# One core, a macaron block (FFN, mLSTM with RG-LRU, FFN): x loaded first, a new ramp, mixer squares on ScalarE, adaLN rates by section, two tiles kept for the end

## The chip, the cores and the metric

One core of one Trainium2 chip. The metric is the device time of one execution in microseconds (us); the core's engines are TensorE (PE in the profile, its weight loads PEld), VectorE (DVE), ScalarE (ACT), GpSimd (POOL) and SyncE (SP, which issues most DMA loads).

## The reference

The input x has 256 rows (tokens) of 2048 float32 values; everything is float32. The block is three sublayers, each modulated by a vector c (adaLN):

```python
mod = (silu(c) @ w_ada + b_ada).reshape(3, 3, 2048)          # shift, scale, gate of each sublayer
def modulate(h, s): return layer_norm(h) * (1 + scale[s]) + shift[s]

y = swiglu(modulate(x, 0), ffn1_w13, ffn1_w2)                # (silu(u@wg) * (u@wv)) @ w2, inner width 5632
x = layer_norm(ALPHA*x + 0.5*gate[0]*y, ln_g[0], ln_b[0])
u = modulate(x, 1)
q, k, v, o, i, f, x_rg, g_rg = split(u @ w_in + b_in)
h_m = layer_norm(mlstm(q, k, v, i, f)) * mlstm_norm_g * sigmoid(o)     # 4 heads of 256
x_rg = causal_depthwise_conv(x_rg, width 4)
h_r = rg_lru(x_rg, ...) * gelu(g_rg)                          # gates in 8 blocks of 128, recurrence over time
y = concat(h_m, h_r) @ w_out
x = layer_norm(ALPHA*x + gate[1]*y, ln_g[1], ln_b[1])
y = swiglu(modulate(x, 2), ffn2_w13, ffn2_w2)
x = layer_norm(ALPHA*x + 0.5*gate[2]*y, ln_g[2], ln_b[2])
```

## The kernel before

**Weights.** Each weight matrix is cut into tiles of 1 MB (128 partitions x 2048 float32). A tile is loaded on SP's queue into one of four `raw` buffers (L86). ScalarE casts it to a rounded `hi` part (L96), VectorE forms `lo` = raw - hi (L98), and each product is three matmuls: hi by hi, lo by hi, hi by lo (L638 to L640 in the ramp, L289 to L291 elsewhere). The tiles' names are `r`, `h` or `l` with a section behind: `rra7`, `hra7`, `lra7` are the three forms of ramp tile 7; `rs` belongs to the mixer's projections, `rv` and `ro` to v and o, `rwo` to the output projection. The hi and lo tiles have three buffers each.

**adaLN.** The product of silu(c) with `w_ada` is done on VectorE: 144 tiles of 1 MB, called `ada0` to `ada143`, are loaded through the same queue and the same four `raw` buffers, and each takes one multiply-and-sum (L174, "the reduce") that leaves 128 numbers of shift, scale or gate in `adac`. They are spread over the program by a rate: each load of a weight tile adds the rate of the section to a credit, and each whole credit loads an adaLN tile (`tick`). Where a value is needed, `ada_until` issues all that lead to it at once. So the constants `RAMP_RATE`, `FFN1_RATE`, `MIX_RATE` and `FFN2_RATE` place these tiles.

**Start and ramp.** x comes in four pieces; VectorE takes the statistics of each half of the rows (`stx`, `mvx`), GpSimd the inverse deviation (`vex`, `rsx`), ScalarE normalizes (`n`, L1092). TensorE transposes 128-column blocks of n (L243, bank `tu`); ScalarE applies scale and shift (L247) and rounds (L250), VectorE forms the low part (L251): that is u, one "k-tile" per 128 columns, 16 in all. The first part of FFN1, the ramp, does 16 units of 512 columns with only the first k-tiles, then with the next, and so on: `STAGES` = (2, 4, 5, 5) k-tiles. A stage of k k-tiles reads 4 k weight tiles. In each stage, `modulate` of the next stage's k-tiles stands ahead of unit 14. Partial sums of units 0 and 1 stay in PSUM (`kp`); the others go to SBUF, by ScalarE copies in stage 0 (L673) and by VectorE adds later (L675).

**Mixer.** After a boundary (final take of y, layer norm, next u) come the sections o, x (with the convolution, L899 and L902), g (the RG gates L910 to L913, the recurrence L919 to L929, its output L937 to L944), v, k, then q with the four heads (L978 to L1016) and the output projection. The heads' decay weights are in `misc`.

**Tail.** After FFN2's last group, `boundary` finishes the two halves of the rows one after the other: `products(t)` adds the last weight tiles into four banks per half (`tl20n`, `tl21n`), `take` multiplies by the gate, adds to x and takes statistics, `norm` writes the layer norm and the output.

**Order.** A scheduler orders each engine's instructions by a simulated timeline; engines wrapped in `Pinned` (V, A, G, T) keep program order.

## Time and profile before

| what | value |
|---|---|
| median of 3 runs | 1959.12 us (1951.45 to 1960.45) |
| the profiled execution | 1956.92 us, its span 1955.1 us |
| TensorE busy | 1881.4 us, 96% |
| VectorE, ScalarE, GpSimd busy | 1425.5, 847.8, 43.3 us |
| granted TensorE clock, mean | 0.988 |
| DMA | 515.87 MB, mean 264 GB/s |

The span runs from the first to the last instruction of the trace. In a row of the timeline the numbers are start and duration in us; a bracket gives the idle time of the engine ahead of the instruction and what ended it. In a group's row they are total busy time and the mean of one in ns, then the idle time before them.

### The profile page before, as it was taken

The page shows a single profiled execution, that of the slowest core. Times are in us where ns is not written, and L with a number is a line of the kernel's source. Part 1 is how long each engine was busy: PE and PEld are TensorE (multiplying, and loading weights), DVE is VectorE, ACT ScalarE, POOL GpSimd, SP SyncE. Part 2 cuts the span into 40 slices and gives each one's busy share as a digit, 9 for nine tenths or more (in the row PEclk, how much of TensorE's full clock was granted, in tenths as well). Part 3 has the DMA queues.
Part 4 walks back from the last instruction along what each step waited for, and adds up shares of the span by engine and source line. Part 5 has one row for each costly group of instructions (what it writes and reads, how often), then busy time and mean ns, then how long its engine had stood idle before and what let it go on. Part 6 is the DMA issues. An engine that isn't in the chain of part 4 may idle for free.

```text
span 1955.1 us, 21210 instructions
## 1 busy us (share of the span) xinstructions
PE 1881.4 (96%) x8571; PEld 1554.9 (80%) x8571; DVE 1425.5 (73%) x1364; ACT 847.8 (43%) x814; POOL 43.3 (2%) x65
## 2 busy tenths in 40 slices
PE   5899999999999999899989898999999999999997
PEld 4788888888888887688878786788888888888885
DVE  6898888978877978699997876555655544545656
ACT  5534344444443345647544246533444333333340
POOL 0000000000000000000000121000000000000000
PEclk9999999999999999899999999999999999999998
DMA  8988877888987984587888663566666555555562
GB/s 335 373 327 320 302 280 291 294 313 312 362 332 294 340 342 196 199 331 291 329 331 338 237 251 137 215 236 244 251 239 257 194 194 190 185 188 211 194 223 78
DMA packets 73203, 515.87 MB, mean 264 GB/s; under 512 B 8545, under 2 KB 8721, under 8 KB 11025
## 3 DMA queue, kind: packets, MB, share of 16 engines
q1 hardware_dynamic: 70848, 507.54, 69.5%
q10 hardware_dynamic: 1728, 3.80, 0.6%
q0 software_dynamic: 528, 3.17, 0.4%
q8 instruction: 67, 1.10, 0.2%
q14 instruction: 32, 0.25, 0.0%
HBM read 512.36 MB, written 2.12 MB: 263 GB/s over the span
## 4 chain that ended last, share of the span: by engine, by line
PE 78%; DVE 9%; DMA 6%; ACT 4%; issue 3%; POOL 0%; DVEq 0%; SPq 0%; ACTq 0%
PE py L290 6%; PE py L289 6%; PE py L291 6%; PE fv L290 5%; PE fv L291 5%; PE fv L289 5%; PE fg L291 5%; PE fg L290 5%; PE fg L289 5%; PE pj L279 5%; DMA ada<-in_w_ada 3%; PE rp L639 3%; PE rp L640 3%; PE rp L638 3%; PE pj L280 2%
## 5 line engine op out<-in xcount | busy, mean ns | idle before, releaser
L174 DVE CUSTOM_DVE_ANT_0 ada<-ada,scb,badac 128x2048 f32<-128x2048 f32 x144 | 337.7, 2345 | 84.1 <-DMA ada<-in_w_ada 83.8
L98 DVE TENSOR_TENSOR lw<-rw,hw 128x2048 fp32r<-128x2048 f32 x80 | 183.1, 2290 | 107.0 <-ACT hw L96 106.8
L96 ACT CAST hw<-rw 128x2048 fp32r<-128x2048 f32 x80 | 153.1, 1914 | 235.2 <-PE py L291 118.6
L98 DVE TENSOR_TENSOR lfv<-rfv,hfv 128x2048 fp32r<-128x2048 f32 x56 | 128.2, 2291 | 126.0 <-ACT hfv L96 125.9
L289 PE MATMUL py<-hw,hth 128*128 128x512 f32 x512 | 199.7, 391 | 0.0
L291 PE MATMUL py<-hw,htl 128*128 128x512 f32 x512 | 199.4, 389 | 0.0
L290 PE MATMUL py<-lw,hth 128*128 128x512 f32 x512 | 199.3, 389 | 0.0
L96 ACT CAST hra<-rra 128x2048 fp32r<-128x2048 f32 (+1 forms) x67 | 122.8, 1837 | 173.0 <-PE rp L640 140.0
L279 PE MATMUL pj<-u,hs 128*128 128x512 f32 x512 | 181.5, 399 | 5.0 <-ACT rh L943 5.0
L98 DVE TENSOR_TENSOR lfg<-rfg,hfg 128x2048 fp32r<-128x2048 f32 x52 | 119.1, 2291 | 88.5 <-ACT hfg L96 88.5
L638 PE MATMUL rp<-hra,u 128*128 128x512 f32 x448 | 172.0, 395 | 5.6 <-ACT hra L96 5.4
L96 ACT CAST hfg<-rfg 128x2048 fp32r<-128x2048 f32 (+1 forms) x56 | 101.7, 1822 | 173.9 <-PE fv L291 73.3
L96 ACT CAST hfv<-rfv 128x2048 fp32r<-128x2048 f32 x56 | 107.1, 1913 | 161.0 <-PE fg L291 124.5
L289 PE MATMUL fv<-hfv,u 128*128 128x512 f32 x448 | 174.7, 391 | 2.3 <-ACT hfv L96 2.3
L290 PE MATMUL fv<-lfv,u 128*128 128x512 f32 x448 | 175.2, 391 | 1.6 <-DVE lfv L98 1.6
L639 PE MATMUL rp<-lra,u 128*128 128x512 f32 x448 | 174.8, 391 | 0.3 <-DVE lra L98 0.3
L291 PE MATMUL fv<-hfv,u 128*128 128x512 f32 x448 | 174.9, 390 | 0.0
L640 PE MATMUL rp<-hra,u 128*128 128x512 f32 x448 | 174.2, 391 | 0.0
L289 PE MATMUL fg<-hfg,u 128*128 128x512 f32 x432 | 169.6, 392 | 0.0
L291 PE MATMUL fg<-hfg,u 128*128 128x512 f32 x432 | 168.9, 391 | 0.0
L290 PE MATMUL fg<-lfg,u 128*128 128x512 f32 x432 | 168.7, 391 | 0.0
L98 DVE TENSOR_TENSOR lra<-rra,hra 128x2048 fp32r<-128x2048 f32 (+1 forms) x67 | 146.7, 2192 | 20.7 <-ACT hra L96 20.7
(374 smaller groups left out, 3453.1 us busy)
## 6 DMA issues: line engine op xcount, KB each, us to landing
ada<-in_w_ada SPq DMA_DIRECT2D x144, 1024.0 KB, 5.5
rw<-in_w SPq DMA_DIRECT2D x80, 1024.0 KB, 4.9
rra<-in_w_r SPq DMA_DIRECT2D x64, 1024.0 KB, 4.9
rfg<-in_w SPq DMA_DIRECT2D x56, 1024.0 KB, 4.9
rfv<-in_w SPq DMA_DIRECT2D x56, 1024.0 KB, 4.9
rs<-in_w_s SPq DMA_DIRECT2D x32, 1024.0 KB, 6.4
rwo<-in_w_out SPq DMA_DIRECT2D x16, 1024.0 KB, 4.8
ro<-in_w_vo SPq DMA_DIRECT2D x8, 1024.0 KB, 4.8
```

What stands on the lines that cost most here:

```text
L96: act.copy(cut(hi, w), like(raw[:, w], hi))
L98: low.tensor_sub(cut(lo, w), like(raw[:, w], lo), cut(hi, w).bitcast(F32))
L174: nc.vector.tensor_tensor_reduce(raw, raw, scb, 1.0, badac[:, s, j, kt:kt + 1], ALU.mult, ALU.add, adac[:, s, j, kt:kt + 1])
L279: nc.tensor.matmul(ps, hi[:, w], u2[:, k].rearrange("p w b -> p (w b)"), start=k == 0, stop=False)
L280: nc.tensor.matmul(ps[:, 0:S], lo[:, w], uh[:, k, :], start=False, stop=k == KT - 1)
L289: nc.tensor.matmul(o, acth[:, k0 + j, tk], cut(hi, w), start=first and j == 0, stop=False)
L290: nc.tensor.matmul(o, acth[:, k0 + j, tk], cut(lo, w), start=False, stop=False)
L291: mm = nc.tensor.matmul(o, actl[:, k0 + j, tk], cut(hi, w), start=False, stop=last and j == 3)
L638: nc.tensor.matmul(pss[t], uh[:, k0 + j, tk], hi[:, w], start=a0 and j == j0, stop=False)
L639: nc.tensor.matmul(pss[t], uh[:, k0 + j, tk], lo[:, w], start=False, stop=False)
L640: mm = nc.tensor.matmul(pss[t], ul[:, k0 + j, tk], hi[:, w], start=False, stop=a1 and j == j0 + nj - 1)
```

## The change

1. The four loads of x come before the first adaLN tile. The statistics, the addition of 1 to the scale's bias and two adaLN reduces are issued on VectorE in program order (`vec` is the pinned engine).
2. The ramp's stages are 2, 3, 4 and 7 k-tiles, with new adaLN rates; FFN1's rate rises from 0.68 to 0.72.
3. The mixer's single rate becomes one per section. By the order of the loads, 50 adaLN tiles lie ahead of the ramp's end (46 before), 96 ahead of FFN1's end (89), 111 ahead of the end of the v section (109), 123 ahead of the first output-projection tile (121).
4. In the mixer, the first tap of the convolution and the squares in the recurrence and the gelu go from VectorE to ScalarE, and three VectorE operations of the gelu (L937 to L939) become one on each engine.
5. At the end, the products of group 9's last two column tiles with the second half of the rows (24 matmuls) are held back until `products(1)`.

```diff
-STAGES = (2, 4, 5, 5)
+STAGES = (2, 3, 4, 7)
-RAMP_RATE = (1.0, 0.63, 0.6, 0.6)
-FFN1_RATE = 0.68
-MIX_RATE = 0.76
+RAMP_RATE = (0.75, 0.67, 0.88, 0.6)
+FFN1_RATE = 0.72
+MIX_RATE = dict(o=0.9, x=0.6, g=0.4, v=0.5, k=0.9, q=0.65, out=0.72)
...
 def g2_kept(gi):
-                for k in range(2):
-                    hl = load_w(w2[(2 * gi + k) * 4 + n], f"w2{s}_{2 * gi + k}_{n}")
+            for k, n in ((0, 0), (1, 0), (0, 1), (1, 1), (0, 2), (0, 3), (1, 2), (1, 3)):
+                hl = load_w(w2[(2 * gi + k) * 4 + n], f"w2{s}_{2 * gi + k}_{n}")
+                if not following and k and n > 1:
+                    mov_t(ps_last[0, n], hl, hth, htl, k * 4, 0, False, False)
+                    behind_t.append((n, hl))
+                else:
                     mov_w([ps_last[t, n] for t in range(NT)], hl, hth, htl, k * 4, k == 0, False)
...
+        def last_tile(ps, t, n):
+            if t:
+                for m, hl in behind_t:
+                    mov_t(ps_last[1, m], hl, hth0, htl0, 4, 1, False, False)
+                behind_t.clear()
+            mov_t(ps, hls[n], hth, htl, 0, t, False, True)
...
 def conv():
-                nc.vector.tensor_scalar(xc[:, n, :], xr[:, n, 0:S], rgp[:, 0, n:n + 1], rgp[:, 4, n:n + 1],
-                                        op0=ALU.mult, op1=ALU.add)
+                nc.scalar.activation(xc[:, n, :], xr[:, n, 0:S], AF.Identity, bias=rgp[:, 4, n:n + 1],
+                                     scale=rgp[:, 0, n:n + 1])
...
 def recurrence():
-                nc.vector.tensor_mul(sq, rr[:, b, :], rr[:, b, :])
+                nc.scalar.activation(sq, rr[:, b, :], AF.Square)
...
 def rg_out():
-                nc.vector.tensor_mul(t2, gg[:, b, :], gg[:, b, :])
-                nc.vector.tensor_scalar(t2, t2, 0.044715, 1.0, op0=ALU.mult, op1=ALU.add)
-                nc.vector.tensor_mul(t2, t2, gg[:, b, :])
+                nc.scalar.activation(t2, gg[:, b, :], AF.Square, scale=float(np.sqrt(0.044715)))
+                nc.vector.scalar_tensor_tensor(t2, t2, 1.0, gg[:, b, :], op0=ALU.add, op1=ALU.mult)
...
 def start():
-        nc.vector.tensor_scalar_add(badac[:, :, 1, :], badac[:, :, 1, :], 1.0)
-        ada_tile()
         for t in range(NT):
             for c in range(0, D, 1024):
                 nc.sync.dma_start(x[:, t, c:c + 1024], a["x"][t * P:(t + 1) * P, c:c + 1024])
-        mom = [moments(stats_of(x[:, t, :], f"x{t}"), f"x{t}") for t in range(NT)]
+        mom = [moments(stats_of(x[:, t, :], f"x{t}", V), f"x{t}", V) for t in range(NT)]
+        V.tensor_scalar_add(badac[:, :, 1, :], badac[:, :, 1, :], 1.0)
+        ada_tile(V)
+        ada_tile(V)
```

Three places of the instruction order follow. First VectorE at the start of the program, before:

```order
L210 BN_STATS stx0_133<-x_110 128x6 x2
L1081 TENSOR_SCALAR badac_112<-badac_112 128x3x16
L210 BN_STATS stx0_133<-x_110 128x6 x2
L215 BN_AGGR mvx0_138<-stx0_133 128x2
L210 BN_STATS stx1_147<-x_110 128x6
L174 ISA ada0_124,adac_113<-ada0_124,scb_82,badac_112 128x2048
L174 ISA adac_113 128x1
L210 BN_STATS stx1_147<-x_110 128x6 x3
L174 ISA ada1_165,adac_113<-ada1_165,scb_82,badac_112 128x2048
L174 ISA adac_113 128x1
L215 BN_AGGR mvx1_152<-stx1_147 128x2
L174 ISA ada2_168,adac_113<-ada2_168,scb_82,badac_112 128x2048
```

and after:

```order
L121 BN_STATS stx0_129<-x_110 128x6 x4
L121 BN_AGGR mvx0_134<-stx0_129 128x2
L121 BN_STATS stx1_143<-x_110 128x6 x4
L121 BN_AGGR mvx1_148<-stx1_143 128x2
L121 TENSOR_SCALAR badac_112<-badac_112 128x3x16
L121 ISA ada0_158,adac_113<-ada0_158,scb_82,badac_112 128x2048
L121 ISA adac_113 128x1
L121 ISA ada1_161,adac_113<-ada1_161,scb_82,badac_112 128x2048
L121 ISA adac_113 128x1
L98 TENSOR_TENSOR lra0_171<-rra0_168,hra0_170 128x512 x4
L251 TENSOR_TENSOR u2_111<-u0_0_183,u2_111 128x256
L174 ISA ada2_207,adac_113<-ada2_207,scb_82,badac_112 128x2048
```

The statistics of both halves now stand together, and the adaLN reduces begin behind them; only two of them stand ahead of the first weight tile's low part.

Second, ScalarE at the end of ramp stage 0, around the cast of weight tile 7 (`hra7`); `tu` are the transposes of the next stage's columns. Before:

```order
L673 COPY x_110<-rp0_131_458 128x512
L247 ACTIVATE u0_2_487<-tu0_2_482,adac_113 128x256 x2
L247 ACTIVATE u0_4_497<-tu0_4_492,adac_113 128x256
L250 CAST u2_111<-u0_2_487 128x2x256
L247 ACTIVATE u0_4_497<-tu0_4_492,adac_113 128x256
L250 CAST u2_111<-u0_4_497 128x2x256
L96 CAST hra7_509<-rra7_507 128x2048
L96 CAST hra8_545<-rra8_543 128x2048
```

and after:

```order
L673 COPY x_110<-rp0_131_455 128x512
L247 ACTIVATE u0_2_481<-tu0_2_476,adac_113 128x256 x2
L247 ACTIVATE u0_4_489<-tu0_4_486,adac_113 128x256
L96 CAST hra7_500<-rra7_498 128x2048
L250 CAST u2_111<-u0_2_481 128x2x256
L250 CAST u2_111<-u0_4_489 128x256
L96 CAST hra8_536<-rra8_534 128x2048
```

The cast moves ahead of the two roundings of u (L250), and there is one application of scale and shift (L247) fewer.

Third, VectorE at the mixer's last head (3), between the decay weights' use of `pm3` and of `pk3`. `lwo` is the low part of an output-projection tile. Before:

```order
L1008 BN_AGGR hmv21_7688<-hst21_7686 128x2
L1011 TENSOR_SCALAR hve20_7670<-hmv20_7668,rd20_7662 128x1
L98 TENSOR_TENSOR lwo00_7884<-rwo00_7881,hwo00_7883 128x2048
L1011 TENSOR_SCALAR hve21_7690<-hmv21_7688,rd21_7682 128x1
L990 SCALAR_TENSOR_TENSOR misc_5651<-pk3_7704,misc_5651 128x384
L1013 TENSOR_TENSOR rsh20_7674<-rsh20_7674,rd20_7662 128x1
```

and after (the same operation on `pk3` is L1006 now):

```order
L997 SCALAR_TENSOR_TENSOR misc_5675<-pm3_7701,gcol_5677,misc_5675 128x128
L1029 TENSOR_TENSOR rsh11_7611<-rsh11_7611,rd11_7599 128x1
L1020 RECIPROCAL rd21_7684<-rd21_7684 128x1
L1032 TENSOR_TENSOR og_5470<-og_5470,pn10_7577 128x256
L1024 BN_AGGR hmv21_7690<-hst21_7688 128x2
L1029 TENSOR_TENSOR rsh20_7676<-rsh20_7676,rd20_7664 128x1
L1031 TENSOR_SCALAR pn11_7596<-pn11_7596,hmv11_7605,rsh11_7611 128x256
L1027 TENSOR_SCALAR hve21_7692<-hmv21_7690,rd21_7684 128x1
L1031 TENSOR_SCALAR pn20_7662<-pn20_7662,hmv20_7670,rsh20_7676 128x256
L1006 SCALAR_TENSOR_TENSOR misc_5675<-pk3_7706,misc_5675 128x384
L1032 TENSOR_TENSOR og_5470<-og_5470,pn11_7596 128x256
```

The low part of the weight tile is gone from the stretch, and small operations of heads 1 and 2 stand there.

## The prediction

> **What bounds the kernel now.** I read the page's busy shares first, then busy time by stage, then the list of waits of TensorE (PE).

> ```profile
> span 1955.1 us, 21210 instructions
> PE 1881.4 (96%) x8571; PEld 1554.9 (80%) x8571; DVE 1425.5 (73%) x1364; ACT 847.8 (43%) x814; POOL 43.3 (2%) x65
> ```

> PE is the bound: a change that removes no matmul can win only from the 1955.1 - 1881.4 = 73.7 us in which PE is idle, and from matmuls that run at a lower granted clock. The stages (interval, its length, then busy time of each engine, PEclk, DMA share, GB/s):

> ```profile
> 0.00:26.65 26.65, 4.60 (x19) 3.65 (x19) 13.99 (x21) 12.36 (x21) 4.28 (x11) 1.00 0.90 357
> 26.65:83.70 57.05, 51.37 (x204) 40.71 (x205) 45.89 (x36) 34.76 (x44) 0.00 (x0) 0.94 0.91 344
> 83.70:172.00 88.30, 88.30 (x396) 73.18 (x395) 81.49 (x70) 35.25 (x27) 0.00 (x0) 1.00 0.90 338
> 172.00:281.50 109.50, 108.23 (x482) 89.37 (x481) 87.38 (x73) 40.89 (x28) 0.00 (x0) 1.00 0.79 290
> 815.00:1010.00 195.00, 192.40 (x1019) 164.91 (x1017) 181.99 (x191) 104.50 (x107) 1.36 (x4) 1.00 0.85 318
> 1930.00:1955.00 25.00, 10.52 (x47) 8.38 (x45) 20.97 (x33) 0.00 (x0) 3.37 (x4) 0.78 0.25 84
> ```

> The first 83.7 us (the start and ramp stage 0) hold 26.65 - 4.60 + 57.05 - 51.37 = 27.7 us of idle PE; the middle stages almost none; the mixer's first part 2.6; the tail 14.5. What PE waited for in the places that the change touches:

> ```profile
> PE tu L243 <- ACT n L1092: 10.9, 2, 8.5
> PE rp L638 <- ACT hra L96: 5.4, 1, 5.4
> PE pn L998 <- DVE misc L990: 5.0, 1, 5.0
> PE pj L279 <- ACT rh L943: 5.0, 1, 5.0
> PE kp L638 <- ACT u L250: 4.1, 1, 4.1
> ```

> **The start (x first, VectorE pinned).** The loads run back to back, and VectorE (DVE) takes adaLN tiles between the statistics of x:

> ```profile
> GB/s 0 0 109 253 418 429 332 243 254 370 437 399 371 410 453 459 404 437 426 426 426 426 426 415 415 448 415 426 415 426 415 426 448 393 142 0 0 0 0 87
> 11.16 0.23 POOL L202 TENSOR_SCALAR vex<-mvx 128x1 f32<-128x1 f32 x1 [9.86 <-DVE mvx L215]
> 18.19 2.19 POOL L202 TENSOR_SCALAR vex<-mvx 128x1 f32<-128x1 f32 x1 [6.15 <-DVE mvx L215]
> 23.67 0.55 ACT L247 ACTIVATE u<-tu,adac 128x256 f32<-128x256 f32 x1
> 26.65 0.80 PE L638 MATMUL kp<-hra,u 128*128 128x512 f32 x1 [4.12 <-ACT u L250]
> ```

> The first row is 0 to 30 us in 40 slices; 426 GB/s is 1.05 MB in 2.46 us. After the change 2 MB of x, two adaLN tiles and weight tile 0 are the first 5 MB; before, weight tile 0 came after 6 MB. The reduces of DVE no longer stand between the two halves' statistics, so the second mean (used by POOL at 18.19) comes some 7 us earlier, and what limits the first u is the reduce of the second adaLN tile. Its load is the fourth MB before as after. The bandwidth row sums (slices of 0.75 us) to 4.2 MB at 13.2 us and to 4.7 MB at 14.5, so I put its landing at 14.5 at the latest; a reduce is 2.35 (rows below), so u can start at 16.9. From u to the first product stands 26.65 - 23.67 = 2.98, in which ACT casts the four pieces of weight tile 0 (the fifth MB, 5.2 MB by the row at 15.7, so there in time): 19.9 in place of 26.65, **-6.7**. Bounds: -4 (a late weight tile: its successor must be cast and subtracted within 6.5 us of the first product, and the new order has a reduce before that too) to -8.5 (the second mean alone sets it).

> POOL's one-element operation takes 0.23 at 11.16 and 2.19 at 18.19, where a reduce ran beside it. [...]

> **The end of stage 0 (two adaLN tiles fewer ahead of weight tile 7).**

> ```profile
> 69.19 1.48 ACT L247 ACTIVATE u<-tu,adac 128x256 f32<-128x256 f32 x3
> 73.03 1.90 ACT L96 CAST hra<-rra 128x2048 fp32r<-128x2048 f32 x1 [0.74 <-DMA rra<-in_w_r]
> 74.98 1.22 PE L638 MATMUL rp<-hra,u 128*128 128x512 f32 x2 [5.43 <-ACT hra L96]
> 74.98:80.45 5.47, 5.22 (x11) 3.64 (x12) 5.27 (x3) 2.48 (x2) 0.00 (x0) 0.50 0.96 355
> 777.14 1.11 PE L121 MATMUL tu<-ident,n 128*128 128x128 f32 x4 [2.35 <-ACT n L121]
> 777.10:782.00 4.90, 4.86 (x17) 4.07 (x18) 4.73 (x8) 4.73 (x11) 0.00 (x0) 0.69 0.00 0
> ```

> Tile 7 landed at 73.03. In the new order 11 adaLN tiles precede it, not 13: 73.0 - 6.7 - 2 x 2.46 = 61.4, so it is no longer late. Late next is ScalarE (ACT): its cast now stands behind the three L247 only, 69.19 + 1.48 - 6.7 = 63.9, and PE started 74.98 - 73.03 = 1.95 after the cast's start: 65.9. PE is there at 74.98 - 5.43 - 6.7 = 62.8, so the gap shrinks from 5.4 to about 3.1: **-2.3** (0, to -5.4 if the cast goes first). After the gap 11 matmuls took 5.22 at a clock of 0.50, about 2.7 lost against 0.226 each; I leave that in.

> [...] After idle of only 2.35 (the 777.14 row) the clock of the next 4.9 us is 0.69. [...]

> Stage 1 thus begins 9.0 us earlier.

> **Ramp stages of 3, 4, 7 and their adaLN rates.**

> ```profile
> L98 DVE TENSOR_TENSOR lra<-rra,hra 128x2048 fp32r<-128x2048 f32 x17 | 38.9, 2287 | 6.5 <-ACT hra L96 6.5
> L174 DVE CUSTOM_DVE_ANT_0 ada<-ada,scb,badac 128x2048 f32<-128x2048 f32 x12 | 28.1, 2344 | 0.0
> L174 DVE CUSTOM_DVE_ANT_0 ada<-ada,scb,badac 128x2048 f32<-128x2048 f32 x11 | 25.9, 2351 | 17.3 <-DMA ada<-in_w_ada 17.3
> L675 DVE TENSOR_TENSOR extra<-extra,rp 128x512 f32<-128x512 f32 x8 | 5.4, 682 | 1.6 <-PE rp L640 1.6
> ```

> (The first, second and fourth are 84 to 172, the third 172 to 270.) PE's matmuls are the same number; stage 1 is 12 weight tiles at 88.3/16 = 5.52 us, 66.2, stage 2 is 16, 88.3. DVE does per stage the lo tiles, the adaLN reduces and 28 adds. Row durations overlap a little (17 x 2.29 + 12 x 2.34 + 27 x 0.68 + 1.8 = 87.2 stands as 81.5 busy), so times 0.935: stage 1 (8 reduces) (27.4 + 18.8 + 19.0 + 1.3) x 0.935 = 62.2 of 66.2; stage 2 (14) (36.6 + 32.8 + 19.0 + 2.2) x 0.935 = 84.7 of 88.3. It fits at 94 and 96%; before it was 92%, with PE never idle. Loads in stage 2: 30 MB x 2.46 = 74 of 88. Cost 0. Into stage 3, seven k-tiles' transposes take four PSUM banks at once instead of three, and an adaLN reduce now stands between the two adds that free them. The 1.27 us of idle in 172 to 281.5 grows by between 0 and 2 x 2.35; one reduce partly under the transposes: **+1.5**. The 3 adaLN tiles more in FFN1's second part cost DVE 7 us in a stretch where it has slack: 0 (cover gone, +7).

> **The mixer.** DVE is 93% busy from 815 to 1010, and PE's 5.0 us wait at its end is this chain:

> ```profile
> 1009.25 1.90 ACT L96 CAST hs<-rs 128x2048 fp32r<-128x2048 f32 x1 [2.05 <-DMA rs<-in_w_s]
> 1012.37:1015.70 3.33, 3.33 (x11) 2.85 (x11) 3.33 (x5) 1.37 (x4) 0.00 (x0) 0.50 0.98 391
> L899 DVE TENSOR_SCALAR xc<-xr,rgp 128x256 f32<-128x256 f32 x8 | 3.2, 398 | 0.0
> L937 DVE TENSOR_TENSOR t<-gg 128x512 f32<-128x512 f32 x4 | 2.7, 673 | 0.0
> L938 DVE TENSOR_SCALAR t<-t 128x512 f32<-128x512 f32 x4 | 1.6, 411 | 0.0
> ```

> The weight tile landed late since its buffer is freed by DVE. The change takes from DVE the 8 L899 (3.2), 4 squares of L924 (as L937, 2.7), L937 and L938 (4.3; L939 stays as a fused one), and 5 adaLN reduces (the order has 15 for 20 by the end of the v section), 5 x 2.35 = 11.8: 22 of 182, which leaves 82%. ACT gains some 16 operations of 0.5 to 0.6, 9 us on 104.5 of 195, and no table load. The wait and the slow clock behind it (11 matmuls in 3.33, 1.4 lost) go: **-6.4** (0 to -6.4). The reduces that go to k, q and out meet a DVE that is less full. In the o section one more reduce stands ahead of lo tiles; if it delays one, PE waits up to 2.35, a loss that I keep for the range.

> **The last head.**

> ```profile
> 1106.33 0.52 ACT L983 ACTIVATE misc<-misc 128x384 f32<-128x384 f32 x1
> 1106.45 2.29 DVE L98 TENSOR_TENSOR lwo<-rwo,hwo 128x2048 fp32r<-128x2048 f32 x1 [0.51 <-ACT hwo L96]
> 1108.85 0.55 DVE L990 SCALAR_TENSOR_TENSOR misc<-pk,misc 128x384 f32<-128x384 f32 x1
> ```

> PE's 5.0 us end with L990, behind a lo tile of 2.29 and an exp that waited for a cast. In the new order neither stands there, but eight small DVE operations do (about 1.7), and four more matmuls (0.9) cover: 5.0 to about 2.3, **-2.7** (0 to -7.5, with the clock).

> **The tail.**

> ```profile
> 1929.68 0.69 DVE L121 TENSOR_TENSOR gy<-tl,gate 128x512 f32<-128x512 f32 x1 [0.57 <-PE tl L291]
> 1937.46 0.68 DVE L121 TENSOR_TENSOR gy<-tl,gate 128x512 f32<-128x512 f32 x1
> 1940.13 0.39 PE L291 MATMUL tl<-u,htl 128*128 128x512 f32 x1
> 1945.77 0.26 DVE L121 BATCH_NORM_AGGREGATE mvp<-sts 128x2 f32<-128x24 f32 x1
> ```

> Of row half 1, 24 matmuls (24 x 0.226 = 5.4) move behind row half 0's last products. PE still ends at 1940.5; half 0's last bank is out 5.4 earlier, its normalization ends by 1932, and the four takes of half 1 follow PE rather than DVE: the last ends 2.05 (a take in 1937.46 to 1945.77, four of them) after 1940.5, 1942.6 for 1945.8: **-3.2** (-2 to -5.4).

> **Sum.** -6.7 - 2.3 + 1.5 - 6.4 - 2.7 - 3.2 = -19.8. The profiled execution took 1956.92: 1937.1. The median of the runs shown, 1959.12, lies 2.2 above it: **1939**.

> **Rivals.** (B) VectorE's queue in stages 1 and 2, at 94 to 96%, stalls PE where a reduce comes just ahead of a lo tile; for it: the 26.65 to 83.70 row, where forced reduces did so. Four stalls of 2.35 give 9.4 back: 1948. Against: no PE idle in 83.7 to 172 at 92%. (C) The mixer's and head's waits stay, since ACT's added squares delay the casts: 1939 + 9.1 = 1948. (D) The clock loss after the shrunken gaps goes too (2.7 + 2.5) and the head's wait (2.3): 1931. [...] (E) Slower: the 22 reduces of stages 1 and 2 wait for their loads as in the third row of that fence, 17.3/11 = 1.57 us each with the queue behind them: 34.5 more on DVE against 7.6 us of slack (154.5 - 146.9), +27: 1966. PE idles from 7.6/22 = 0.35 a reduce on, and the change is slower than before from (19.8 + 7.6)/22 = 1.25. The clock after such gaps, as in the 777.10 row (4.9 x 0.31 = 1.5 for a gap of 2.35), adds up to 17 more: 1966 to 1983, most of it over 1968.9, the line of slower. Against: 0.0 for the twelve at 84 to 172, where DVE was as full; DVE idled for loads only where it had slack. (F) Nothing that lasts: the early gain becomes waits at FFN1's loads, 1957.

> **Chances.** The forecast (1933 to 1946) 0.52, B 0.14, C 0.13, D 0.11, E 0.06, F 0.04. A measurement of this kernel can tell about 0.5%, 9.8 us: faster means under 1949.3. B and C lie near that line, so a quarter of each counts as no change, with F: faster 0.52 + 0.11 + 0.20 = 0.83, same 0.07 + 0.04 = 0.11, slower 0.06 (E). Range 1928 (D, with the head's whole 7.5) to 1951 (B and C, with the scatter of the runs); what lies outside is E, F and the rare case of B and C together.

> **What would show it.** First product near 20; PE's gap before tile 7 near 3 with its cast behind L247; no wait on rh L943; a gap of 2 to 3 before the last head's products; DVE's last aggregate 2 us after PE's end. Wrong if PE idles within 75 to 270 by more than 5 us, or a new wait on hs or lra appears in the mixer.

## The result, and the profile after

The changed kernel takes 1936.71 us (median of 4 runs, 1933.5 to 1939.1) where the kernel before took 1959.78 on the same chip: ratio 0.989, interval 0.9857 to 0.9922. The forecast was 1939 within 1928 to 1951, and faster. The profiled execution took 1939.1, its span is 1937.3, 17.8 less than before.

The profile page's first lines, then busy time by stage (the same stages as before, moved to where they now lie; columns as ahead):

```profile
span 1937.3 us, 21222 instructions
PE 1879.3 (97%) x8571; PEld 1551.7 (80%) x8571; DVE 1416.4 (73%) x1344; ACT 855.7 (44%) x830; POOL 38.1 (2%) x65
```

```profile
0.00:20.17 20.17, 4.33 (x19) 3.60 (x19) 12.28 (x19) 12.19 (x20) 2.31 (x11) 0.80 0.90 355
20.17:75.40 55.23, 50.50 (x198) 40.03 (x199) 43.92 (x35) 34.16 (x43) 0.00 (x0) 0.89 0.92 357
75.40:141.60 66.20, 65.52 (x294) 54.16 (x293) 63.55 (x59) 26.62 (x20) 0.00 (x0) 1.00 0.94 343
141.60:230.00 88.40, 87.69 (x394) 72.40 (x393) 82.75 (x72) 34.89 (x27) 0.00 (x0) 1.00 0.91 343
1916.00:1937.30 21.30, 9.75 (x44) 7.72 (x42) 15.30 (x24) 0.00 (x0) 1.68 (x2) 0.84 0.29 98
```

PE is busy 2.1 us less and idle 15.7 us less (58.0 for 73.7), so the gain is idle time in the main. The first product comes at 20.17 and not 26.65. Ramp stages 1 and 2 hold 0.7 us of idle PE each, with VectorE at 96% (63.55 of 66.2) and 94% (82.75 of 88.4). The clock of 0.89 in ramp stage 0 cannot be set against the 0.94 of the same stage before: that trace holds no clock record ahead of 32.6 us, and such time is shown as 1.00. The first 13 matmuls took 5.35 us there, from 26.65, and take 5.48 us now, from 20.17, at a recorded 0.50. What PE waited for:

```profile
PE kp L638 <- ACT u L250: 6.5, 1, 6.5
PE tu L243 <- ACT n L1111: 4.0, 2, 2.7
PE po L290 <- DVE lo L98: 3.4, 1, 3.4
PE rp L638 <- ACT hra L96: 3.2, 1, 3.2
PE rp L638 <- ACT u L247: 2.4, 3, 1.3
PE pn L1014 <- DVE misc L1006: 1.1, 1, 1.1
```

The wait on `rh` has no row any more, the one on `misc` is 1.1 where it was 5.0, the one on weight tile 7 is 3.2 where it was 5.4. The 6.5 for the first product was 4.1, but with the transposes' waits (4.0 for 10.9) PE's whole start is shorter. New is a wait on scale and shift (L247), 2.4 in three places.

The start, by the timeline:

```profile
11.31 0.22 POOL L202 TENSOR_SCALAR vex<-mvx 128x1 f32<-128x1 f32 x1 [2.45 <-DVE badac L121]
14.73 2.35 DVE L121 CUSTOM_DVE_ANT_0 ada<-ada,scb,badac 128x2048 f32<-128x2048 f32 x1
17.18 0.56 ACT L247 ACTIVATE u<-tu,adac 128x256 f32<-128x256 f32 x1 [2.25 <-DVE adac L121]
20.17 0.79 PE L638 MATMUL kp<-hra,u 128*128 128x512 f32 x1 [6.48 <-ACT u L250]
29.29 0.50 PE L638 MATMUL rp<-hra,u 128*128 128x512 f32 x1 [1.30 <-ACT u L247]
```

The second half's mean is with GpSimd at 11.31 (18.19 before), its operation takes 0.22 and not 2.19 (no reduce beside it: the first begins at 12.27; before, one ran from 18.02 to 20.30), and u waits for the second adaLN reduce, which ends at 17.1. The last row is one of the new waits: the second k-tile's scale comes from a reduce that stands behind weight tile 1's low part.

The end of stage 0, and the tail:

```profile
63.74 1.48 ACT L247 ACTIVATE u<-tu,adac 128x256 f32<-128x256 f32 x3
65.10 1.91 ACT L96 CAST hra<-rra 128x2048 fp32r<-128x2048 f32 x1
67.06 2.08 PE L638 MATMUL rp<-hra,u 128*128 128x512 f32 x4 [3.18 <-ACT hra L96]
67.06:72.53 5.47, 5.21 (x11) 3.65 (x12) 5.47 (x5) 3.17 (x5) 0.00 (x0) 0.50 0.77 283
1925.36 0.39 PE L291 MATMUL tl<-u,htl 128*128 128x512 f32 x1
1927.96 0.26 DVE L121 BATCH_NORM_AGGREGATE mvp<-sts 128x2 f32<-128x24 f32 x1
```

The cast's row has no idle time ahead of it and no wait for a DMA: tile 7 is there, and ScalarE comes to it from L247. After the gap of 3.18 the clock is 0.50, as after 5.43 before. At the end the last aggregate stands 2.6 after PE's last matmul began (5.6 before).

Lined up at the same instructions, the lead over the kernel before is: first product 6.5; ramp tile 7 7.9; FFN1's boundary 7.0; the wait on `lo` in the o section 7.0; the last head's products 16.2; FFN2's first products (L447) 17.6; 35 us further 14.8; PE's last matmul 14.8; the end 17.8.

### The profile page after: what moved, and what is told of

It is laid out like the page before. It is cut to its first block, busy times and chain, and to the rows that moved or that the text cites. A ratio compares the mean times of both kernels' runs of the same rounds, so it can differ in the third digit from the quotient of the medians.

```text
span 1937.3 us, 21222 instructions
## 1 busy us (share of the span) xinstructions
PE 1879.3 (97%) x8571; PEld 1551.7 (80%) x8571; DVE 1416.4 (73%) x1344; ACT 855.7 (44%) x830; POOL 38.1 (2%) x65
## 4 chain that ended last, share of the span: by engine, by line
PE 89%; DVE 4%; ACT 3%; DMA 1%; issue 1%; POOL 0%; SPq 0%; DVEq 0%; ACTq 0%
PE py L291 6%; PE py L289 6%; PE py L290 6%; PE pj L279 5%; PE fv L290 5%; PE fv L291 5%; PE rp L639 5%; PE fv L289 5%; PE rp L638 5%; PE rp L640 5%; PE fg L291 5%; PE fg L289 5%; PE fg L290 5%; PE pj L280 3%; PE tl L290 2%; PE tl L289 2%
## 5 line engine op out<-in xcount | busy, mean ns | idle before, releaser
L174 DVE CUSTOM_DVE_ANT_0 ada<-ada,scb,badac 128x2048 f32<-128x2048 f32 x142 | 333.1, 2348 | 63.5 <-DMA ada<-in_w_ada 63.3
L96 ACT CAST hw<-rw 128x2048 fp32r<-128x2048 f32 x80 | 153.1, 1914 | 236.0 <-PE py L291 128.7
L98 DVE TENSOR_TENSOR lw<-rw,hw 128x2048 fp32r<-128x2048 f32 x80 | 182.8, 2290 | 98.3 <-ACT hw L96 98.2
L98 DVE TENSOR_TENSOR lfv<-rfv,hfv 128x2048 fp32r<-128x2048 f32 x56 | 128.4, 2292 | 135.6 <-ACT hfv L96 135.6
L291 PE MATMUL py<-hw,htl 128*128 128x512 f32 x512 | 199.3, 389 | 0.0
L96 ACT CAST hra<-rra 128x2048 fp32r<-128x2048 f32 (+1 forms) x67 | 122.8, 1838 | 166.3 <-PE rp L640 129.7
L98 DVE TENSOR_TENSOR lfg<-rfg,hfg 128x2048 fp32r<-128x2048 f32 x52 | 119.1, 2291 | 89.1 <-ACT hfg L96 89.1
L279 PE MATMUL pj<-u,hs 128*128 128x512 f32 x512 | 180.0, 397 | 0.0
L96 ACT CAST hfv<-rfv 128x2048 fp32r<-128x2048 f32 x56 | 107.1, 1913 | 161.5 <-PE fg L291 121.8
L96 ACT CAST hfg<-rfg 128x2048 fp32r<-128x2048 f32 (+1 forms) x56 | 101.7, 1822 | 173.2 <-PE fv L291 73.3
L638 PE MATMUL rp<-hra,u 128*128 128x512 f32 x448 | 172.4, 395 | 5.6 <-ACT hra L96 3.2
L291 PE MATMUL fv<-hfv,u 128*128 128x512 f32 x448 | 175.5, 392 | 0.0
L640 PE MATMUL rp<-hra,u 128*128 128x512 f32 x448 | 174.0, 391 | 0.0
L291 PE MATMUL fg<-hfg,u 128*128 128x512 f32 x432 | 168.2, 389 | 0.0
L98 DVE TENSOR_TENSOR lra<-rra,hra 128x2048 fp32r<-128x2048 f32 (+1 forms) x67 | 146.6, 2194 | 27.2 <-ACT hra L96 27.2
```

The source lines that it names most:

```text
L96: act.copy(cut(hi, w), like(raw[:, w], hi))
L98: low.tensor_sub(cut(lo, w), like(raw[:, w], lo), cut(hi, w).bitcast(F32))
L174: vec.tensor_tensor_reduce(raw, raw, scb, 1.0, badac[:, s, j, kt:kt + 1], ALU.mult, ALU.add, adac[:, s, j, kt:kt + 1])
L279: nc.tensor.matmul(ps, hi[:, w], u2[:, k].rearrange("p w b -> p (w b)"), start=k == 0, stop=False)
L291: mm = nc.tensor.matmul(o, actl[:, k0 + j, tk], cut(hi, w), start=False, stop=last and j == 3)
L638: nc.tensor.matmul(pss[t], uh[:, k0 + j, tk], hi[:, w], start=a0 and j == j0, stop=False)
```

## The experiments

Each run is the changed kernel with one edit, against the kernel before on the same chip. To be compared with them, the changed kernel itself once more:

**after_again** (no edit).

> The changed kernel once more, unaltered, as the measure for the runs beside it. Theory: the waits of TensorE stand where they stood, within 0.1 us each, and the time differs from the first profile by what the granted clock does after short gaps: in the six profiles so far the stretch from the wait at the second boundary's last transposes to the third FFN2 tile took 32.3 or 35.1 us with the same instructions. Rival (that stretch depends on the kernel): it repeats its 35.2.

Measured: 1938.26 us, ratio 0.9908 (0.9891 to 0.9926). PE waits 6.49 for the first product, 3.18 for tile 7 and 1.12 at the last head, as in the first profile. Not all waits stood within 0.1 us, as the theory had it: 1.86 stands for 1.21 at the first boundary, 2.70 for 3.35 on `lo`, 1.26 for 0.53 on `lv`, and the wait of 2.24 on u at 1183.46 is gone. The clock differed too. From the FFN2 wait at L447 to its next tile it is 18.89 us (18.83 in the first profile, 17.18 in the kernel before), and 31.14 for the 120 matmuls behind it (32.40; 31.17 before). Of these two parts of FFN2's first tiles the first repeated and the second did not, so neither theory nor rival holds as stated. The last section sets the clock records beside these times.

**old_start**:

```diff
         nc.scalar.dma_start(badac..., a["b_ada"])
+        nc.vector.tensor_scalar_add(badac[:, :, 1, :], badac[:, :, 1, :], 1.0)
+        ada_tile()
...
-        mom = [moments(stats_of(x[:, t, :], f"x{t}", V), f"x{t}", V) for t in range(NT)]
-        V.tensor_scalar_add(badac[:, :, 1, :], badac[:, :, 1, :], 1.0)
-        ada_tile(V)
-        ada_tile(V)
+        mom = [moments(stats_of(x[:, t, :], f"x{t}"), f"x{t}") for t in range(NT)]
```

> The changed kernel with the start as it was before (one adaLN tile loaded ahead of x, VectorE's start ordered by the scheduler), all else changed. Theory (the terms add): the first product returns from 20.2 to about 26.6 us; the small wait of 1.3 at 29.3 (second k-tile's scale) goes, so stage 1 begins about 5 later and the whole takes about 1942. Rival (stage 0 is bound by its loads, so an earlier first product only waits at weight tile 7): the wait before tile 7 shrinks by what the start loses, stage 1 begins at most 2 later, 1937 to 1939.

Measured: 1940.52, ratio 0.9924 (0.9909 to 0.9939), 2 to 4 over the changed kernel; the intervals of the ratios overlap. Its first product and its tile 7:

```profile
23.90 0.79 PE L638 MATMUL kp<-hra,u 128*128 128x512 f32 x1 [2.18 <-ACT u L250]
68.75 0.79 PE L638 MATMUL rp<-hra,u 128*128 128x512 f32 x1 [3.18 <-ACT hra L96]
```

Neither as stated: the start moves by 3.7 only, since with the new rate of stage 0 fewer adaLN tiles crowd it in the old order too. (The third reduce, which ran beside GpSimd's operation at 18.19 before, is not there, and the operation takes 0.22 us at 18.14.) Of the 3.7, 1.7 is left at tile 7, within the rival's 2. But the wait there is the same 3.18 and has not shrunk, so stage 0 is not bound by that load. What makes up the difference is the wait of 1.3 at 29.29, of which 0.4 is left here, and the clock: PE works 2.9 us at 0.50 here (23.90 to 26.76) and 5.5 us in the changed kernel (20.17 to 25.65).

**old_ramp**:

```diff
-STAGES = (2, 3, 4, 7)
-RAMP_RATE = (0.75, 0.67, 0.88, 0.6)
-FFN1_RATE = 0.72
+STAGES = (2, 4, 5, 5)
+RAMP_RATE = (1.0, 0.63, 0.6, 0.6)
+FFN1_RATE = 0.68
```

> The changed kernel with stages 2, 4, 5, 5 and the old rates of the ramp and FFN1. Theory: tile 7 again lands behind two more adaLN tiles, the wait before it is 5.4 for 3.2, the idle at the entry of stage 3 returns to 1.3 for 0.7, the two waits of 1.4 in all on u (134.8 and 221 us) go: +2 at FFN1's start, and the mixer has 7 adaLN tiles more to do, partly on a full VectorE: 1938 to 1943. Rival (the new stages' fuller VectorE costs as much as they win): no later than 1936.7, with PE's idle in 75 to 230 gone.

Measured: 1950.13, ratio 0.9965 (0.9954 to 0.9977): 12 to 13 over the changed kernel, more than either theory.

```profile
69.87 0.79 PE L638 MATMUL rp<-hra,u 128*128 128x512 f32 x1 [4.46 <-ACT hra L96]
1186.40 0.90 PE L121 MATMUL tu<-ident,n 128*128 128x128 f32 x3 [6.55 <-DVE n L121]
```

Tile 7 costs 2.8, the way from there to FFN1's end another 4, and the second boundary 6. With the old rates 124 adaLN tiles are loaded by the rate ahead of that boundary and 128 are needed for the next modulation, so tiles 125 to 128 are loaded one behind the other from 1135.6 to 1147.3, ahead of the last four output-projection tiles. VectorE then comes to the last take ahead of the boundary's first normalization at 1175.3, right behind three low parts of weight tiles; in the changed kernel it is there early and waits 2.83 us for PE (1163.0). The rates of all sections are one budget, which I had overlooked.

**old_stages** keeps the budget:

```diff
-STAGES = (2, 3, 4, 7)
-RAMP_RATE = (0.75, 0.67, 0.88, 0.6)
+STAGES = (2, 4, 5, 5)
+RAMP_RATE = (0.75, 0.7, 0.75, 0.55)
```

> The changed kernel with the ramp's stages back at 2, 4, 5, 5 and rates of 0.75, 0.7, 0.75, 0.55, which leave the same number of adaLN tiles (50, 96, 111, 123) ahead of the ends of ramp, FFN1, v and the projections; so the shape of the stages is tried alone, where the earlier run of the old ramp also pushed four tiles into the second boundary. Theory: the wait before tile 7 is 3.8 to 4.5 for 3.2 (one transposed column more), the waits of 0.7 and 0.5 on u go, 1.1 comes at 264: within 2 us of the changed kernel. Rival (the stage shape is what brought the gain of the ramp): 6 or more slower.

Measured: 1939.74, ratio 0.9906 (0.9884 to 0.9928): not to be told from the changed kernel. The wait at tile 7 is 6.4 (more than expected: its load lands late, the cast at 68.53 waits 1.13 us for it), the waits on u at 135 and 221 are gone, and at FFN1's boundary it stands at 767.2 for 766.5. The shape of the stages brings nothing that these runs can tell; the 10 us between this run and old_ramp are the rates'.

**old_mixer**, **old_squares** and **old_rates**: both mixer edits undone, and each alone. The edits:

```diff
 old_rates, old_mixer
-MIX_RATE = dict(o=0.9, x=0.6, g=0.4, v=0.5, k=0.9, q=0.65, out=0.72)
+MIX_RATE = dict(o=0.76, x=0.76, g=0.76, v=0.76, k=0.76, q=0.76, out=0.76)
 old_squares, old_mixer (and the first tap and recurrence's square alike)
-                nc.scalar.activation(t2, gg[:, b, :], AF.Square, scale=float(np.sqrt(0.044715)))
-                nc.vector.scalar_tensor_tensor(t2, t2, 1.0, gg[:, b, :], op0=ALU.add, op1=ALU.mult)
+                nc.vector.tensor_mul(t2, gg[:, b, :], gg[:, b, :])
+                nc.vector.tensor_scalar(t2, t2, 0.044715, 1.0, op0=ALU.mult, op1=ALU.add)
+                nc.vector.tensor_mul(t2, t2, gg[:, b, :])
```

> The changed kernel with the mixer as before: the first tap and the squares on VectorE, one rate of 0.76 in all its sections. Theory: VectorE is full again from 815 to 1010, the wait of 5.0 at the change from v to k (on rh) comes back with its slow clock of 1.4, and the last head's wait goes back from 1.1 to between 2 and 5: 1943 to 1947. Rival (the 7 adaLN tiles done before the mixer would have been enough): the rh wait stays below 1, 1937 to 1939.

> The changed kernel with the first tap and the squares back on VectorE; the rates by section stay new. Theory (VectorE's total load in 800 to 1000 is what made the wait on rh: 182 of 195 before, 172 of 200 now): 10.2 us come back to VectorE, it is at about 91%, and the rh wait returns in part, 1 to 4 us: 1939 to 1942. Rival (the five adaLN tiles moved out were enough): no rh wait, 1937.

> The changed kernel with one rate of 0.76 in all mixer sections; the tap and the squares stay on ScalarE. Theory: five adaLN tiles come back into the stretch up to the end of v, 11.8 us of VectorE, about 92%, the rh wait returns in part, 1 to 4 us: 1939 to 1942. Rival (the squares alone were enough): no rh wait, 1937, and the last head's wait as now at 1.1.

Measured: old_mixer 1949.88 (0.9963, 0.995 to 0.9976), old_squares 1935.68 (0.9893, 0.9872 to 0.9914), old_rates 1942.03 (0.9933, 0.9912 to 0.9954). Waits of PE in old_mixer:

```profile
PE pn L1015 <- DVE misc L1007: 5.0, 1, 5.0
PE pj L279 <- ACT rh L956: 4.9, 1, 4.9
```

in old_squares and in old_rates:

```profile
PE pn L1015 <- DVE misc L1007: 0.8, 1, 0.8
```

```profile
PE pn L1014 <- DVE misc L1006: 4.7, 1, 4.7
PE pj L279 <- ACT ii L926: 1.5, 1, 1.5
```

and the stage from 801 to 1001 in old_mixer, old_squares, old_rates and the changed kernel:

```profile
801.00:1001.00 200.00, 198.13 (x1033) 168.62 (x1031) 186.23 (x197) 103.19 (x107) 1.36 (x4) 0.99 0.86 321
```

```profile
801.00:1001.00 200.00, 198.29 (x1031) 169.65 (x1032) 182.18 (x198) 106.30 (x113) 1.36 (x4) 0.98 0.79 295
```

```profile
801.00:1001.00 200.00, 197.16 (x1022) 168.11 (x1023) 182.70 (x186) 115.71 (x130) 1.36 (x4) 0.98 0.85 319
```

```profile
801.00:1001.00 200.00, 198.19 (x1029) 169.07 (x1030) 172.33 (x178) 115.74 (x130) 1.36 (x4) 0.98 0.78 292
```

Either edit alone removes the `rh` wait, so the part that both theories expected back (1 to 4 us) did not come, and both rivals were right on it. VectorE (third busy column) is busy for 182 of 200 us where the wait is gone and for 186 where it stands. The rates alone remove the last head's wait, which the rival of old_rates had not expected. With the old rates the low part of an output-projection tile (`lwo`) runs between the uses of `pm3` and `pk3`; with the new ones it does not, squares or no squares. In old_rates:

```profile
1094.55 2.29 DVE L98 TENSOR_TENSOR lwo<-rwo,hwo 128x2048 fp32r<-128x2048 f32 x1
1097.29 0.55 DVE L1006 SCALAR_TENSOR_TENSOR misc<-pk,misc 128x384 f32<-128x384 f32 x1
```

So the squares bring nothing on top of the rates: old_squares is as fast as the changed kernel. The profile of old_mixer is the fastest of its 8 runs (1945.02), so 5 of the 12 by which its median lies higher are not explained by these rows.

**old_tail**: the two tiles multiplied with both halves in their old place.

```diff
-            for k, n in (... (0, 2), (0, 3), (1, 2), (1, 3)):
+            for k, n in (... (0, 2), (1, 2), (0, 3), (1, 3)):
-                if not following and k and n > 1:
+                if False:
```

> The changed kernel with the last group's two column tiles of the second row half done in their old place, ahead of the first half's last products. Theory: TensorE ends where it does now, VectorE ends 3.0 later, since the first half's normalization runs 5.4 later and pushes the second half's takes: 1939.7. Rival (the end is set by the output's write, not VectorE): no change.

Measured: 1941.97, ratio 0.9927 (0.9914 to 0.9941). PE's last matmul began at 1924.60, and

```profile
1930.24 0.26 DVE L121 BATCH_NORM_AGGREGATE mvp<-sts 128x2 f32<-128x24 f32 x1
```

stands 5.64 after it, against 2.60 in the changed kernel: 3.0 for the edit, as expected. The time is 4 to 5 over the changed kernel; what is more than 3.0 is within the scatter of the runs.

**both**, **o3** and **early7b** try what is left: the wait of 3.35 on `lo` in the o section, and the 3.18 before tile 7.

```diff
 all three
-                credit[:] = -2.0, MIX_RATE['o']
+                credit[:] = -3.0, MIX_RATE['o']
 both
-                    if q == units - 2 and not last:
+                    if q == units - (3 if first else 2) and not last:
 early7b
                 for q in range(units):
+                    if first and q == units - 3:
+                        tile_of((units - 2) * k // 4)
```

> The changed kernel with two further edits: in ramp stage 0 the next stage's transposes stand ahead of unit 13 in place of unit 14, and the mixer's credit begins at -3 in place of -2, so that the first adaLN reduce comes behind two low parts of the o section. Theory: ScalarE has applied scale and shift before weight tile 7 lands at 62.1, its cast goes at once, and PE's wait of 3.2 there falls to 0.3 with the 2.7 lost at the slow clock behind it; the wait of 3.35 on lo falls to about 1 with up to 2.9 at the slow clock: 8 us less than the changed kernel, 1929. Rival (what is late next takes the place: the two adaLN tiles forced there, and the second boundary's own chain): 3 us or less, 1934.

> The changed kernel with the mixer's credit beginning at -3 in place of -2 and nothing else. Theory: the whole gain of the run with two edits (its ramp was level with the changed kernel's by 135 us) is this one: the wait on lo near 802 is 1.1 for 3.3 and the clock behind it stays up, 4 less than the changed kernel, 1933 to 1934. Rival: part of it came from the moved transposes, 1936.

> The changed kernel with the mixer's credit at -3 as in the run with two edits, and in ramp stage 0 weight tile 7 asked for ahead of unit 13, before the adaLN tiles 9 and 10 (the transposes stay at unit 14). Theory: tile 7 lands near 58, its cast runs before the copies of unit 12 and 13, PE's wait of 3.2 at 67 and the slow clock behind it go: at tile 8 it is 3 to 6 ahead of the changed kernel, and with the o section's 4 the whole is 1929 to 1932. Rival (adaLN tile 9 is late instead, and stage 1's first k-tile 4 with it): a wait of 2 to 4 on u at tile 8 or 9, the ramp gains under 1: 1933.

Measured: both 1932.75 (0.9885, 0.9865 to 0.9905), o3 1934.86 (0.9883, 0.986 to 0.9906), early7b 1926.69 (0.9848, 0.9824 to 0.9872).

In o3:

```profile
PE po L290 <- DVE lo L98: 1.1, 1, 1.1
```

In the run called both, the transposes are early, but the order puts the cast behind the copies of unit 13 all the same:

```profile
64.13 0.59 ACT L673 COPY x<-rp 128x512 f32<-128x512 f32 x1 [0.49 <-PE rp L640]
64.61 3.70 ACT L96 CAST hra<-rra 128x2048 fp32r<-128x2048 f32 x2
66.57 1.47 PE L638 MATMUL rp<-hra,u 128*128 128x512 f32 x4 [2.47 <-ACT hra L96]
```

The wait is 2.5 and 0.9, and at 135 us nothing is left of it: the rival's case, and all of its gain is o3's. In early7b the tile itself is asked for earlier:

```profile
58.25 1.91 ACT L96 CAST hra<-rra 128x2048 fp32r<-128x2048 f32 x1
60.00:75.00 15.00, 15.00 (x70) 12.46 (x70) 12.40 (x10) 10.85 (x17) 0.00 (x0) 1.00 0.93 359
75.00:230.00 155.00, 154.33 (x686) 126.59 (x685) 152.66 (x137) 63.01 (x46) 0.00 (x0) 1.00 0.92 353
```

The wait is gone, the clock stays at 1.00, the next k-tile is not late, and FFN1's boundary begins at 760.8 (766.5). This is the fastest version measured: 31 us less than the kernel before, 10 to 12 less than the changed one, and 2 to 5 less than expected. In its profile PE's last matmul comes 12.7 us earlier than in the changed kernel's first profile; 2.6 of these lie in FFN2's first tiles; the last section sets such differences beside the clock records. In its second row VectorE is busy for 152.66 of 155 us and PE idles 0.7.

## Why the prediction was right, step by step

- **Start**, -6.7: 6.5. The step was right in its working: the second reduce ended at 17.1 (16.9 forecast), the first product came 2.99 after u's beginning (2.98). Not seen was the 1.3 at 29.29. But not all of it is the start edit's work: without that edit 3.7 of the 6.5 goes at the first product, and at tile 7 only 1.7 of the lead of 7.9; without the new ramp and its rates 2.8 of the 7.9 goes. Either edit alone had most of it.
- **Tile 7**, -2.3: the cast stood behind L247, the gap is 3.18 for 3.1, and stage 1 came 7.9 earlier for 9.0, short by 1.1, most of which is the wait of 1.3 at 29.29. The clock behind the gap was 0.50; the forecast had left that loss in, on the strength of the row at 777.14 (0.69 behind a gap of 2.35).
- **Stages**, cost 0 and +1.5: the wrong sign at stage 3's entry, 0.7 for 1.3, not 2.8. I let the add that frees the last bank wait out a whole reduce; PE waited for L247 there. With 0.7 at stage 2's entry the sum of these waits is +0.1; from tile 7 to FFN1's boundary, with the clock behind tile 7, the lead falls by 0.9. VectorE's 94 and 96% came out as 96 and 94%, and PE did not starve: rival E's price never fell due.
- **Mixer and head**, -9.1: from the `lo` wait to the last head's products the stretch is 291.3 for 300.5, -9.2. That the total fits so well is luck in part, for errors in it cancel. Lined up at the same instructions, the lead falls from 7.0 to 5.5 ahead of the `rh` wait's place (two waits of 0.4 and 0.5 are new, and 0.6 more is lost), stands at 12.2 behind it, and at 16.2 at the last head's products. So the `rh` term is 6.7 for 6.4, the head 4.1 for 2.7 (its gap was mis-sized, 1.1 for 2.3), and 1.5 was lost that had no term. The cause was half wrong. I took 22 us from VectorE for this; about 10, by either edit, is enough, and the squares are not needed at all. ScalarE's table loads stayed at 12, of 1.28 us each, as the forecast had it. I also read the wait as the late weight tile's, whose cast ends at 1011.15. What PE waited for last was `rh`, and that stood behind a reduce on VectorE:

```profile
1008.66 2.35 DVE L174 CUSTOM_DVE_ANT_0 ada<-ada,scb,badac 128x2048 f32<-128x2048 f32 x1
1010.93 0.69 DVE L942 SCALAR_TENSOR_TENSOR t<-t,xc 128x512 f32<-128x512 f32 x1
1011.65 0.62 ACT L943 CAST rh<-t 128x512 fp32r<-128x512 f32 x1 [0.50 <-DVE t L942]
```

- **Tail**, -3.2: 3.0, by the forecast's chain.
- **Not in the sum**: behind the head the clock stayed at 1.00 (0.65 in the same 7.55 us before), which with a new wait of 0.7 at 1108.68 gained 1.4; rival D had counted on that clock. In FFN2's first tiles 2.9 was lost, 1.65 and 1.23 in two stretches; the clock stood at 0.50 for 3.41 us more in each. So the profile's span fell by 17.8 where the terms gave 19.8, and the median by 23.1, since the profiled execution is the slowest of the four. The forecast's 1939 for 1936.7 is as good as that allows, and some of its nearness is luck.

## What to carry to other kernels

Credit that is shared by sections is one budget: here a rate lowered in one place came back as four forced loads at a later deadline, so an edit of one rate is best tried with the totals held. It also means that the edits undone one at a time (2 to 4, 12 to 13, 12 to 13 and 4 to 5 us) add up to more than the 23 us of all together, and are not shares of it. Where a cast stood late in ScalarE's order, asking for its tile one unit earlier did more (early7b) than moving the transposes ahead of it (both). Of several ways to relieve a busy engine one may do, so each is worth a run alone. The share of busy time does not tell by itself whether an engine stalls its neighbour: VectorE at 93% did in the mixer, and at 98% in early7b's ramp it did not. In both of the mixer's waits it was one long operation (a reduce, a low part) that stood ahead of the one that PE waited for.

## What was not expected of the hardware

In these traces the clock after a short gap does not go with the gap alone. The same instructions at the second boundary, after waits of 2.38 and 2.37, before and after:

```profile
1195.60:1201.00 5.40, 5.00 (x16) 3.71 (x16) 2.81 (x6) 2.56 (x8) 0.56 (x1) 0.68 0.40 130
```

```profile
1177.70:1183.00 5.30, 3.42 (x16) 2.57 (x16) 2.81 (x6) 2.46 (x8) 0.56 (x1) 1.00 0.37 121
```

At 0.68 the 16 matmuls took 5.0 us, at 1.00 3.4. Nothing was lost by it here, since PE waits for u behind them, 0.7 us before and 2.2 after: from the one wait's end to the next it is 5.66 and 5.67 us.

```profile
1193.17:1196.58 3.41, 1.03 (x8) 1.00 0.00 0
1196.58:1200.00 3.42, 3.42 (x9) 0.50 0.33 81
```

```profile
1175.94:1179.36 3.42, 1.57 (x9) 1.00 0.00 0
1179.36:1182.77 3.41, 1.85 (x9) 1.00 0.52 161
```

Before, the wait of 2.38 lies in one cell, and the next cell has the half clock. After, a border falls into the wait, the two cells have 1.85 and 1.56 us of idle PE, and the clock stays at 1.00. From 40 us on, each of the 86 cells at full clock in which PE was idle for more than 1.9 us was followed by a cell at 0.50, and none of the 6974 with less than 1.6 us was; 17 lie between, with either outcome. In the profiles before and after taken alone it is 13 of 13, none of 1067, and 1 of the 4 between. That is what these traces show; no run tried the gap or its place by itself.

From FFN2's L447 to its next tile the thirteen profiles show 17.2 (eight) or 18.7 to 18.9 (five). The wait ahead of it does not tell them apart: 2.27 stands in both groups. A cell at 0.50 does: the five have one in that stretch, the eight have none. The 120 matmuls behind it take 29.8 without such a cell (one profile), 30.9 to 31.4 with one and 32.0 to 32.9 with two. So the two stretches together take 48.1 to 51.2 us with the same instructions, and a difference of up to 3 us between two single profiles there goes with the number of cells at 0.50.
